# Two chained transformer blocks on one core: the fourth PSUM bank in the dense expert stage, the table store on GpSimd's queue, and the order of the first gates

## The chip, the cores and the metric

One core of one Trainium2 chip runs the whole program in a single launch. The metric is the device time of that launch in microseconds (us). All arithmetic is float32; products are made as three passes on values split into a high and a low part ("fp32r" in the rows).

## The reference, cut to what matters

Two blocks follow each other on 512 tokens of width 1024. The first has a gated linear attention branch, a sparse attention branch and a layer of 16384 experts (PEER); the second has a pooling mixer and a stick-breaking attention. The change lies in PEER:

```
s1, s2 = scores of q against 128 sub keys each
v1, i1 = top_k(s1, 16); v2, i2 = top_k(s2, 16)
best, ci = top_k(v1[..., :, None] + v2[..., None, :], 16)
expert_idx = ia * 128 + ib
gates = softmax(best)
u = expert_u[ix]; v = expert_v[ix]
a = gelu(einsum('td,thkd->thk', hx, u)) * gx
y = einsum('thk,thkd->td', a, v)
```

Each token thus uses 8 x 16 of the 16384 experts.

## The kernel before, in words

**Dense and sparse part.** For tokens 0 to 383 the expert layer is computed densely: all 16384 experts, as 128 chunks of 128 experts, with a table of gates that is zero where an expert wasn't chosen. For the last 128 tokens the chosen rows of `uv` are fetched by an indirect DMA and used on VectorE, one of 128 (head, rank) pairs at a time. The sparse part is called "rows" below.

**The gate table** (`peer_table`, lines 1414 to 1468). Four tokens at a time (a quad, 96 in all), VectorE and GpSimd make two one-hot matrices (L1422 to L1430), TensorE multiplies them (L1442), and ScalarE copies the 128 x 128 gates of each token into a stage of 64 tokens (L1445). A stage is 4 MB, 16 quads fill one, and there are six. Two buffers take turns, so a stage is written into the buffer of the one before the last. A full stage is stored to DRAM (`G`). The quads are made four items ahead of their product (`lag`). Between the quads stand hidden products whose results are stored for later ("spilled", `hidden` in the rows; L1485 copies one out of PSUM, ScalarE's queue stores it).

**The dense stage** (`peer`, lines 1634 to 1705). The chunks are worked in 32 groups of four. A chunk's gate step (`gate_chunk`, lines 1508 to 1524) applies Gelu to the hidden values in a PSUM bank (L1515 when they were spilled and are read from SBUF, L1518 when TensorE has just made them), multiplies by the gates (L1519), makes the high part (L1522), and later the low part (L1524, put off through `lowers`). Then eight output products (`peer_out`, lines 1530 to 1561), of twelve matmuls each, multiply the four chunks by `v`, and VectorE adds each to its sum (L1554 the first time, L1556 after). In most groups two of the four chunks are spilled and two are made on the spot, with 24 matmuls each; in groups 0, 6, 13, 19 and 26 all four are spilled. The outputs of a group are worked between the gate steps of the next one.

A row step (`step`, lines 1593 to 1609) goes with each chunk: L1600 adds a row's `v` part to a sum, `lowers` brings L1524, L1608 multiplies the next row's `u` part. Every third group has one step more. L1583 fetches the rows, two steps ahead, on GpSimd's queue.

**Banks.** Two PSUM tiles of two banks each hold the rows' operands in this stage. The others are 0, 1, 6 and 7. `self.ring(out=[...])` sets the list that `bank("out")` walks through in order, starting again at its first; a gate step and an output product each take the next. Before the change the list is 0, 1, 7 in the whole dense stage; bank 6 is used once, for chunk 6 (`early`).

**Order of the work.** Nothing is scheduled by the compiler: each engine runs its instructions in the order in which the items issue them, and waits where it needs data or a free buffer. `run` (lines 383 to 450) walks through the items. Ahead of each item it issues the casts of its weights and of `split_ahead` units behind them (L428 on ScalarE, the high part; L429, mostly on GpSimd, the low part), as far as there is room for three units, and right after each cast it issues the load of a following unit on SP's queue (two buffers). So a cast stands in ScalarE's order in front of the item that it was issued with, and a load stands in SP's order in front of the fetches that the item makes. `fetch_gates` (lines 1496 to 1506) loads a chunk's gates, and its spilled values, on SP's queue, four chunks ahead; it needs the whole table stored.

```
upto, n = last + 1, 0
while upto < len(units) and n < self.split_ahead:
    n += units[upto].split
    upto += 1
split(last + 1, upto)
...
it.fn(*[u.hl if u.split else u for u in it.units])
```

The transition goes like this: last quads and last table store, five more spilled products, `rows_banks` (row fetches 0 to 2) and `fetch_gates(4)` in front of them, then the product of chunk 6, the gates of chunks 0 to 3 and of chunk 6, then the first outputs.

Of the kernel before, what the change touches and what calls it, by code (L numbers as in the profile page):

```python
# [23 lines left out]
ND = NT - P  # L24
# [6 lines left out]
W = 64  # L31
# [258 lines left out]
def weave(main, fill):  # L290

    if not fill:
        return list(main)
    out = []
    tm = sum(i.cost for i in main) or 1.0
    tf = sum(i.cost for i in fill) or 1.0
    cm = cf = 0.0
    a, b = list(main), list(fill)
    while a or b:
        if a and (not b or cm / tm <= cf / tf):  # L300
            i = a.pop(0)
            cm += i.cost
        else:
            i = b.pop(0)
            cf += i.cost
        out.append(i)
    return out


class K:  # L310
# [1103 lines left out]
    def peer_table(self, first, fill):  # L1414

        nc, A = self.nc, self.A
        st = {}

        def quad(n):
            t0 = 4 * n  # L1420
            oa, ob = self.tmp(4 * P), self.tmp(4 * P)
            nc.vector.tensor_tensor(ob.v(4, P), self.iota[:, None, :].to_broadcast([P, 4, P]),  # L1422
                                    self.ibT.v(ND)[:, t0:t0 + 4, None].to_broadcast([P, 4, P]), op=OP.is_equal)
            if n % 2:
                nc.vector.tensor_tensor(oa.v(4, P), self.iota[:, None, :].to_broadcast([P, 4, P]),
                                        self.iaT.v(ND)[:, t0:t0 + 4, None].to_broadcast([P, 4, P]), op=OP.is_equal)
                nc.gpsimd.tensor_mul(oa.v(4, P), oa.v(4, P), self.gT.v(ND)[:, t0:t0 + 4, None].to_broadcast([P, 4, P]))
            for j in range(0 if n % 2 else 4):
                t = slice(t0 + j, t0 + j + 1)
                nc.vector.tensor_scalar(oa.v(4, P)[:, j], self.iota, self.iaT.v(ND)[:, t], self.gT.v(ND)[:, t],  # L1430
                                        op0=OP.is_equal, op1=OP.mult)
            st[n] = (oa, ob)

        def outer(n):
            oa, ob = st.pop(n)
            t0 = 4 * n
            if t0 == W:
                st["buf"] = A.wide.alloc(P * W, high=False, name="stage")
            stage = (st["buf"] if t0 // W % 2 else self.rows).v(P, W)
            ps = self.bank("out")  # L1440
            for j in range(4):
                nc.tensor.matmul(ps[:, j * P:j * P + P], lhsT=oa.v(4, P)[:, j], rhs=ob.v(4, P)[:, j], start=j == 0, stop=True,  # L1442
                                 skip_group_check=True)
            o = t0 % W
            nc.scalar.copy(stage[:, :, o:o + 4].rearrange("p b t -> p t b"), ps.rearrange("p (t b) -> p t b", b=P))  # L1445
            self.free(oa, ob)
            if o + 4 == W:
                self.load(self.G[:, t0 // W], stage, nc.scalar)
            if n == ND // 4 - 1:
                self.free(st["buf"])  # L1450
                self.free(self.gT, self.iaT, self.ibT)
                A.new_wide("split")

        items = []
        lag = 4
        for n in range(ND // 4 + lag):
            def fn(n=n):
                if n >= lag:
                    outer(n - lag)
                if n < ND // 4:  # L1460
                    quad(n)
            items.append(Item(fn, (), 0.9))
            if n == lag - 1:
                items += first
            if n >= lag and (n - lag) % 4 == 3 and n < ND // 4 and n - lag not in (27, 59):
                items += fill[:1]
                del fill[:1]
        return items + fill
# [165 lines left out]
    def peer(self, table, late):  # L1634
        nc, A = self.nc, self.A
        groups = P // 4
        ahead = []
        for gi in range(groups - 1):
            ahead += list(range(4 * gi, 4 * gi + (4 if gi in (0, 6, 13, 19, 26) else 2)))
        fresh = [c for c in range(P) if c not in ahead]  # L1640
        self.spilled = {c: i for i, c in enumerate(ahead)}
        self.order = []
        for gi in range(groups):
            self.order += [4 * gi + i for i in ((0, 2, 1, 3) if gi > 1 else (2, 0, 1, 3) if gi else range(4))]
        rows = self.dram.tile([P, P * ND + 1024], F32, name="gates")
        self.G = rows[:, :P * ND].rearrange("p (g b t) -> p g b t", b=P, t=W)
        self.H = self.dram.tile([len(ahead), P, ND], F32, name="hidden")
        self.g_bufs, self.act, self.g_next, self.lower = {}, {}, 0, []
        self.spare = []
        keys = self.peer_keys()  # L1650
        hid = self.peer_hidden(ahead, True)

        def begin():
            self.pacc = FRows(self, KB, name="pacc")

        def reload():
            self.x2 = FRows(self, KB, name="x2", slots=True)
            for i in range(KB):
                self.load(self.x2[:, i], self.X[i])
        n1 = len(ahead) - table  # L1660
        soft, turn = self.peer_gates()
        h = n1 - late
        items = weave(keys, hid[:h]) + hid[h:n1 - 4] + soft + hid[n1 - 4:n1 - 2]
        items.append(self.rings_at(hid=[6, 7], out=[0, 1, 2, 3, 4], att=[0, 1]))
        items += turn + self.peer_table(hid[n1 - 2:n1], hid[n1:])
        end = len(items) - 5
        items[end:end] = [self.rings_at(hid=[6, 7], out=[0, 1, 6, 7]), Item(self.rows_banks, (), 0.0),
                          Item(lambda: self.fetch_gates(4), (), 0.0)]
        items += [Item(begin, (), 0.0), Item(lambda: self.free(*self.spare), (), 0.0)]
        rest = dict(zip(fresh, self.peer_hidden(fresh, False)))  # L1670
        items += [self.rings_at(out=[6]), rest[6], self.rings_at(out=[0, 1, 7])]
        for c in range(4):
            items.append(Item(lambda c=c: (self.gate_chunk(c), self.lowers()), (), 0.0))
        items.append(Item(lambda: (self.gate_chunk(6, self.early), self.lowers()), (), 0.0))
        sparse = self.peer_rows()
        out = self.peer_out()
        pend = []
        for gi in range(groups):
            if gi == groups - 1:
                for a, b in sparse:  # L1680
                    items += [a, b]
                items.append(Item(reload, (), 0.0))
                sparse = []
            for i in range(4):
                c = self.order[4 * gi + i]
                n = 1 if gi else 0
                now, sparse = sparse[:n], sparse[n:]
                if c > 3 and c != 6:
                    items.append(rest[c] if c in rest else Item(lambda c=c: self.gate_chunk(c), (), 0.0))
                items += [a for a, _ in now] or [Item(self.lowers, (), 0.0)]  # L1690
                items += pend[2 * i:2 * i + 1]
                items += [b for _, b in now]
                items += pend[2 * i + 1:2 * i + 2]
                if i == 1 and gi and gi % 3 == 0:
                    items += sparse[0]
                    sparse = sparse[1:]
            if gi == groups - 1:
                items.append(Item(self.rows_end, (), 0.0))
            pend = out[gi]
        items += [self.split_by(nc.vector)] + pend  # L1700

        def end():
            self.free(self.pacc)
        items.append(Item(end, (), 0.0))
        return items
# [535 lines left out]
```

## Time and profile before

| | us |
|---|---|
| median of 3 runs | 2870.11 (2868.93 to 2875.13) |
| profiled execution, its own time | 2872.01 |
| its span, first to last instruction | 2870.3 |
| TensorE busy | 2706.1 (94%) |
| VectorE busy | 1746.1 (61%) |
| ScalarE busy | 1254.4 (44%) |
| GpSimd busy | 1609.4 (56%) |
| mean granted TensorE clock | 0.977 of full speed |

The span is cut into stages by what the engines do: up to 960 us the attention branches, the scores and the expert choice; 960 to 1130 the table; 1130 to 1185 the transition; 1185 to 2032 the dense stage; from then on the second block. PE is TensorE, DVE VectorE, ACT ScalarE, POOL GpSimd, SP SyncE; a q behind a name is that engine's instruction queue, where DMAs are issued. L1519 is line 1519 of the kernel; L380 is the helper that issues a DMA. An arrow reads "output tile<-input tiles"; in brackets stands the idle time of the engine before the instruction and what ended it.

### The profile page before, as it was taken

Reading aid. Unit: us, or ns where it says so; the run is one execution under the profiler, and the core shown is the slowest. Engines: PE = TensorE matmul, PEld = TensorE weight load, DVE = VectorE, ACT = ScalarE, POOL = GpSimd, SP = SyncE. Lnnn points to the kernel's source line nnn. Section 1 sums busy time; section 2 is a strip of 40 time slices with the busy share of each in tenths; the row PEclk is TensorE's granted clock in tenths of the full one; section 3 lists DMA queues with packets and bytes.
Section 4 is the critical chain, followed back from the end, with each engine's and each line's share of the span. In section 5 each row is a group of like instructions: output and inputs, shape, how many; then the busy total and the mean of one; then the engine's idle time right before and its main releaser. Section 6 shows DMA issues by size and latency. Waiting matters only on the chain.

```text
span 2870.3 us, 40036 instructions
## 1 busy us (share of the span) xinstructions
PE 2706.1 (94%) x14514; PEld 2443.0 (85%) x14514; DVE 1746.1 (61%) x3546; ACT 1254.4 (44%) x2507; POOL 1609.4 (56%) x1503
## 2 busy tenths in 40 slices
PE   6999999999999999798998989989999999999997
PEld 5897788888999999798998989889888887888896
DVE  6334576686888885466666676665584532444655
ACT  4344525534333575344443443434443234445543
POOL 3000334356777755476766667666655554766774
PEclk9999999999999999899999999999999999999998
DMA  6221221284344566789889898897323222221210
GB/s 245 89 74 59 88 78 41 81 324 146 134 148 141 193 242 241 255 315 332 315 312 336 299 326 327 302 342 253 118 87 118 88 103 74 74 74 59 74 59 30
DMA packets 187447, 502.19 MB, mean 175 GB/s; under 512 B 110192, under 2 KB 128752, under 8 KB 138864
## 3 DMA queue, kind: packets, MB, share of 16 engines
q1 hardware_dynamic: 151328, 305.04, 31.7%
q0 software_dynamic: 19072, 136.32, 11.7%
q10 hardware_dynamic: 16848, 58.27, 5.3%
q8 instruction: 114, 1.87, 0.3%
q14 instruction: 85, 0.70, 0.1%
HBM read 456.06 MB, written 43.52 MB: 174 GB/s over the span
## 4 chain that ended last, share of the span: by engine, by line
PE 38%; DMA 6%; DVE 5%; ACT 5%; POOL 3%; issue 2%; DVEq 0%; POOLq 0%; SPq 0%; ACTq 0%
PE bank L370 13%; PE bank L371 12%; PE bank L372 12%; DMA plain<-in_uv_dram,slot 5%; ACT split L428 2%; POOL split L429 2%; DVE bank L1600 1%; DVE bank L1519 1%; DVE plain L1608 1%; PE bank L2017 1%; PE bank L2016 1%; ACT bank L1518 0%; DVE slot L2001 0%; DVE slot L1556 0%; DVE wide L1524 0%
## 5 line engine op out<-in xcount | busy, mean ns | idle before, releaser
L429 POOL TENSOR_TENSOR split<-raw,split 128x512 fp32r<-128x512 f32 x856 | 1096.8, 1315 | 717.9 <-ACT split L428 637.5
L370 PE MATMUL bank<-slot,split 128*128 128x384 f32 (+2 forms) x1932 | 709.6, 367 | 38.8 <-DVE wide L1524 28.2
L371 PE MATMUL bank<-slot,split 128*128 128x384 f32 (+2 forms) x1932 | 703.1, 364 | 0.3 <-DVE slot L377 0.2
L372 PE MATMUL bank<-slot,split 128*128 128x384 f32 (+2 forms) x1932 | 702.8, 364 | 0.0
L370 PE MATMUL bank<-wide,split 128*128 128x384 f32 (+1 forms) x1688 | 620.7, 368 | 76.4 <-DVE slot L1556 27.6
L371 PE MATMUL bank<-wide,split 128*128 128x384 f32 (+1 forms) x1688 | 611.2, 362 | 2.2 <-POOL wide L629 2.2
L372 PE MATMUL bank<-wide,split 128*128 128x384 f32 (+1 forms) x1688 | 610.1, 361 | 0.0
L428 ACT CAST split<-raw 128x512 fp32r<-128x512 f32 x953 | 523.0, 619 | 138.2 <-PE bank L371 71.6
L370 PEld LDWEIGHTS bank<-slot,split 128*128 128x128 f32 (+1 forms) x1932 | 368.1, 191 | 82.1 <-DVE wide L1524 31.1
L370 PEld LDWEIGHTS bank<-wide,split 128*128 128x128 f32 x1688 | 323.7, 192 | 126.7 <-ACT slot L1605 23.3
L371 PEld LDWEIGHTS bank<-slot,split 128*128 128x128 f32 (+1 forms) x1932 | 368.2, 191 | 36.2 <-DVE slot L377 1.1
L372 PEld LDWEIGHTS bank<-slot,split 128*128 128x128 f32 (+1 forms) x1932 | 367.3, 190 | 36.1
L371 PEld LDWEIGHTS bank<-wide,split 128*128 128x128 f32 x1688 | 323.7, 192 | 30.6 <-POOL wide L629 3.4
L372 PEld LDWEIGHTS bank<-wide,split 128*128 128x128 f32 x1688 | 323.4, 192 | 26.9
L1519 DVE TENSOR_TENSOR bank<-bank,slot 128x384 f32<-128x384 f32 x128 | 72.0, 562 | 251.2 <-ACT bank L1518 197.5
L1608 DVE SCALAR_TENSOR_TENSOR plain<-plain,bank 128x1024 f32<-128x1024 f32 x128 | 155.3, 1213 | 80.4 <-DMA plain<-in_uv_dram,slot 80.3
L1583 POOL DMA_INDIRECT plain<-in_uv_dram,slot x128 | 121.3, 948 | 73.3 <-PE bank L371 30.1
L1600 DVE SCALAR_TENSOR_TENSOR bank<-plain,slot,bank 128x1024 f32<-128x1024 f32 x127 | 162.3, 1278 | 0.0
L1518 ACT ACTIVATE bank<-bank 128x384 f32<-128x384 f32 x56 | 26.6, 475 | 304.0 <-PE bank L372 304.0
L1522 ACT CAST wide<-bank 128x384 fp32r<-128x384 f32 x128 | 61.5, 480 | 172.9 <-DVE bank L1519 172.9
L1556 DVE TENSOR_TENSOR slot<-slot,bank 128x384 f32<-128x384 f32 x240 | 124.5, 548 | 15.9 <-PE bank L372 15.9
L429 DVE TENSOR_TENSOR split<-raw,split 128x512 fp32r<-128x512 f32 x97 | 66.2, 743 | 100.4 <-ACT split L428 100.4
(364 smaller groups left out, 3858.1 us busy)
## 6 DMA issues: line engine op xcount, KB each, us to landing
raw<-in_u_dram SPq DMA_DIRECT2D x64, 1024.0 KB, 5.1
raw<-in_v_dram SPq DMA_DIRECT2D x64, 1024.0 KB, 5.4
slot<-gates SPq DMA_DIRECT2D x128, 192.0 KB, 9.6
plain<-in_w_ada_dram ACTq DMA_DIRECT2D x32, 512.0 KB, 6.1
raw<-in_w_pool_dram SPq DMA_DIRECT2D x16, 1024.0 KB, 4.9
slot<-hidden SPq DMA_DIRECT2D x72, 192.0 KB, 10.4
gates<-plain ACTq DMA_DIRECT2D x3, 4096.0 KB, 13.4
gates<-wide ACTq DMA_DIRECT2D x3, 4096.0 KB, 13.0
```

The costliest lines, as they stand in the source:

```text
L370: mm(out, lhsT=w[0], rhs=x[0], start=start, stop=False, skip_group_check=True)
L371: mm(out, lhsT=w[0], rhs=x[1], start=False, stop=False, skip_group_check=True)
L372: mm(out, lhsT=w[1], rhs=x[0], start=False, stop=stop, skip_group_check=True)
L428: self.nc.scalar.copy(u.hl.hi[:, c], u.raw.v(u.n)[:, c])
L429: (u.lo or self.lo_engine).tensor_sub(u.hl.lo[:, c], u.raw.v(u.n)[:, c], u.hl.hi[:, c])
L1519: nc.vector.tensor_mul(ps, ps, b.v(ND))
L1522: nc.scalar.copy(a.hi, ps)
L1556: nc.vector.tensor_add(acc, acc, ps)
L1583: self.nc.gpsimd.indirect_dma_start(out=self.uvs[k % 4].rearrange("p a b -> p (a b)"), out_offset=None, in_=self.t["uv"], in_offset=bass.I ...
L1600: nc.vector.scalar_tensor_tensor(acc, v, a, acc, op0=OP.mult, op1=OP.add)
L1608: nc.vector.scalar_tensor_tensor(u, u, 1.0, self.hx, op0=OP.mult, op1=OP.mult, accum_out=self.dx.v(P)[:, k:k + 1])
L2016: mm(o, lhsT=w, rhs=s["L"][j].hi, start=False, stop=False, skip_group_check=True)
```

## The change

The store of a full stage moves from ScalarE's queue to GpSimd's and is issued three quads later (the last one at once). In the last six table items and up to the gates of chunk 6, weights are cast one unit ahead instead of two. The gates of chunks 0 to 3 are issued in front of the product of chunk 6. After the gates of chunk 6, bank 6 joins the list of the dense stage, which has four banks then.

```diff
             if o + 4 == W:
-                self.load(self.G[:, t0 // W], stage, nc.scalar)
+                st["full"] = (t0 // W, stage)
+            if o == 8 and t0 > W or n == ND // 4 - 1:
+                g, full = st["full"]
+                self.load(self.G[:, g], full, nc.gpsimd)
...
         rest = dict(zip(fresh, self.peer_hidden(fresh, False)))
-        items += [self.rings_at(out=[6]), rest[6], self.rings_at(out=[0, 1, 7])]
+
+        def ahead_by(n):
+            self.split_ahead = n
+        items.insert(end - 6, Item(lambda: ahead_by(1), (), 0.0))
+        items.append(self.rings_at(out=[0, 1, 7]))
         for c in range(4):
             items.append(Item(lambda c=c: (self.gate_chunk(c), self.lowers()), (), 0.0))
-        items.append(Item(lambda: (self.gate_chunk(6, self.early), self.lowers()), (), 0.0))
+        items += [self.rings_at(out=[6]), rest[6], Item(lambda: ahead_by(2), (), 0.0)]
+        items += [Item(lambda: (self.gate_chunk(6, self.early), self.lowers()), (), 0.0), self.rings_at(out=[0, 1, 6, 7])]
```

## Rows read from the trace of the kernel before

**Rows 1.** Windows by stage: length, busy us (instructions) of five engines, PEclk, DMA share, GB/s

```profile
960.00:1130.00 170.00, 169.76 (x1245) 169.57 (x1244) 139.43 (x315) 119.76 (x158) 106.66 (x95) 1.00 0.57 218
...
1130.00:1185.00 55.00, 37.37 (x186) 36.27 (x185) 9.97 (x19) 16.03 (x33) 17.02 (x15) 0.84 0.85 299
...
1185.00:2032.00 847.00, 774.71 (x4258) 754.30 (x4256) 543.17 (x878) 350.41 (x855) 563.59 (x478) 0.97 0.86 309
```

**Rows 2.** Timeline of TensorE in the transition: start us, us, instruction, [idle before <-releaser]

```profile
1155.52 0.69 PE L370 MATMUL bank<-slot,split 128*128 128x384 f32 x1 [4.58 <-ACT slot L1485]
...
1170.56 0.69 PE L370 MATMUL bank<-wide,split 128*128 128x384 f32 x1 [8.62 <-DVE wide L1524]
...
1180.85 0.69 PE L370 MATMUL bank<-wide,split 128*128 128x384 f32 x1 [4.43 <-DVE slot L1554]
```

**Rows 3.** Timeline of the other engines in the transition

```profile
1148.64 0.38 SPq L380 DMA_DIRECT2D slot<-gates  x1
...
1155.47 2.58 SPq L380 DMA_DIRECT2D raw<-in_v_dram  x2
...
1163.25 2.18 ACT L428 CAST split<-raw 128x512 fp32r<-128x512 f32 x4 [7.78 <-DMA raw<-in_v_dram]
...
1163.94 4.93 POOL L429 TENSOR_TENSOR split<-raw,split 128x512 fp32r<-128x512 f32 x4 [6.25 <-ACT split L428]
...
1168.90 0.33 SPq L380 DMA_DIRECT2D raw<-in_u_dram  x1
...
1177.52 0.57 DVE L1519 TENSOR_TENSOR bank<-bank,slot 128x384 f32<-128x384 f32 x1 [3.87 <-DMA slot<-gates]
```

**Rows 4.** The tile `gates` up to 1135 us: issue ns min/median/max, first and last start

```profile
L380 ACTq DMA_DIRECT2D gates<-plain x3: 326/326/327, 983.7 to 1099.1; - x3
L380 ACTq DMA_DIRECT2D gates<-wide x3: 326/326/327, 1010.4 to 1129.9; - x3
...
DMA to landing us min/median/max: 11.5/13.2/18.7
```

**Rows 5.** Waits of TensorE, 1185 to 2032 us: us in total, times, longest

```profile
PE bank L370 <- DVE wide L1524: 28.2, 9, 4.1
PE bank L370 <- DVE slot L1556: 27.6, 29, 5.1
PE bank L370 <- ACT bank L1515: 8.6, 25, 0.3
PE bank L370 <- ACT slot L1605: 6.8, 2, 5.4
```

**Rows 6.** Timeline of TensorE in ordinary groups of the dense stage

```profile
1203.64 0.33 PE L370 MATMUL bank<-slot,split 128*128 128x384 f32 x1
...
1207.80 0.33 PE L370 MATMUL bank<-wide,split 128*128 128x384 f32 x1
...
1281.76 0.41 PE L370 MATMUL bank<-wide,split 128*128 128x384 f32 x1 [0.34 <-ACT bank L1515]
...
1294.82 0.41 PE L370 MATMUL bank<-wide,split 128*128 128x384 f32 x1 [0.34 <-DVE slot L1556]
```

**Rows 7.** Timeline in a group with an extra row step, and in one without hidden products

```profile
1405.26 1.22 DVE L1608 SCALAR_TENSOR_TENSOR plain<-plain,bank 128x1024 f32<-128x1024 f32 x1 [2.59 <-DMA plain<-in_uv_dram,slot]
...
1408.67 0.45 PE L370 MATMUL bank<-slot,split 128*128 128x384 f32 x1 [3.11 <-DVE wide L1524]
...
1517.52 0.66 PE L370 MATMUL bank<-wide,split 128*128 128x384 f32 x1 [5.11 <-DVE slot L1556]
```

**Rows 8.** Windows right after two of the waits for L1524 (columns as in rows 1)

```profile
1408.60:1412.40 3.80, 3.73 (x12) 3.73 (x13) 2.08 (x5) 0.00 (x0) 0.77 (x1) 0.55 1.01 409
...
1492.40:1499.20 6.80, 6.70 (x25) 6.70 (x26) 2.12 (x5) 0.00 (x0) 0.81 (x1) 0.61 1.04 389
```

**Rows 9.** Line L1583, the row fetches: issue ns, who waited (us, times), landing us

```profile
L1583 POOL DMA_INDIRECT plain<-in_uv_dram,slot x128: 936/951/1069, 1127.9 to 1976.8; - x128
...
  DVE plain L1608: 80.3, 39
...
DMA to landing us min/median/max: 7.5/8.6/22.6
```

## Prediction, made before the changed kernel was run

> **What bounds the kernel now.** I first read busy time by stage [rows 1]. While the table is built TensorE is busy 169.76 of 170 us: whatever the change does there can cost time but give none. From 1130 to 1185 us it is busy 37.37 of 55 us, at a granted clock of 0.84. In the dense stage, 1185 to 2032 us, it is busy 774.71 of 847 us. So the change has two places to act: the transition, and 72 us of idle time plus some low clock in the dense stage.
>
> In the transition TensorE stands still three times [rows 2]: 4.58, 8.62 and 4.43 us. The other engines say why [rows 3]. The last 4 MB table store is issued at 1129.9 [rows 4]. The first gate fetch on SP, which needs it landed, goes out at 1148.64. Eight fetches take SP until 1155.47, and only then are the next weights (`w_v`) asked for. ScalarE meanwhile sits in front of the cast of those weights for 7.78 us, and the first Gelu comes after that cast. Then SP holds the fetch of the fifth gates behind a weight load (1168.90), and VectorE waits 3.87 us for it.
>
> In the dense stage nearly all waits are on a PSUM bank [rows 5]: 71.2 us in 65 waits. By the single waits, nine are for L1524 (28.2 us), four are long (5.4, 5.1, 4.5, 4.5), six are of 0.7 to 1.6 us (7.9 us), and 46 are of 0.34 us (15.6 us). Where ScalarE is named, a VectorE eviction ended at the same moment; I read those as bank waits too. The ring has three banks and a group takes twelve, so a product waits for the evacuation three takes earlier. With four it waits for the one four takes earlier. VectorE evacuates in take order, so every such wait moves to an earlier VectorE instruction: **no bank wait can become later through the ring itself.**
>
> **Part 1, the fourth bank.** Pitch: 24 matmuls from 1203.64 to 1207.80 us [rows 6], 4.16 us, so 0.173 us each, and a product of twelve holds a bank for 2.08 us. This is the slack that a fourth bank adds.
>
> *Short waits.* Two of them stand 13.06 us apart [rows 6] with 72 matmuls between (one hidden product, four outputs): 72 x 0.173 = 12.48, so one costs 0.58 us, with its restart, and at least its 0.34 of idle. The eviction it waits for stands in VectorE's order behind L1608, the row product. The one needed with four banks is the L1524 in front of it, or one eviction earlier. All 46 go: 46 x 0.5 = 23 us (16 to 27).
>
> *Waits for L1524.* Every third group has an extra row step. VectorE waits in it for its row (2.59 us), so the gate's L1524 comes late, and the hidden product that wants the gate's bank waits 3.11 us [rows 7]. With four banks that product wants a bank evicted two products before, and the gate's bank goes to an output 4.16 us later. All nine waits are at most 4.1 us, so all fit. The next row then comes late instead: between 0 and 2.08 us each, and I take 0.7, nearer to the lower end because most rows of this stage are there when wanted (39 waits in 128, rows 9). So 28.2 - 6.3 = 22 us. After such a wait the clock falls to its lower level, 1.2 of 2.4 GHz: a granted 0.55 over 3.80 us, or 0.61 over 6.80 [rows 8], which loses 1.7 or 2.7 us. Four of the nine waits are followed by the shorter kind and two by the longer: 4 x 1.7 + 2 x 2.7 = 12 us come back.
>
> *Long and middle waits.* The four long ones are in groups without new hidden products, where VectorE waits for a row (one is 5.11 us, rows 7). A bank buys 2.08 us of each, 8 us; the six middle ones go, 8 us. Together 16 us; I leave their clock as it is.
>
> *Given back.* Rows come by latency: 8.6 us from issue to landing, issued between weight casts on GpSimd [rows 9]. If the stage loses 73 us (23 + 22 + 12 + 16) in 124 rows, each row is wanted 0.6 us sooner. The 39 steps that already wait would wait 23 us more, and others that are just in time begin to. VectorE has slack for part of it: 0 to 35 us, and I take 18. The DMA share of 0.86 [rows 1] would rise to some 0.93, so transfers hide this no worse than now.
>
> Dense stage: 23 + 22 + 12 + 16 - 18 = **55 us**.
>
> **Part 2, the store.** Taken off ScalarE: six issues of 0.33 us, off the path. Put on GpSimd: six issues, at about the 0.95 us of a row fetch, in a stage where TensorE is at 100%. Five of them wait for nothing, because their buffer was full three quads before; behind each on GpSimd stand gate multiplies and casts, which shift by that microsecond. A buffer is written again one stage after its store. Stores are (1129.9 - 983.7) / 5 = 29.2 us apart [rows 4], three quads are 5.5 us, a landing is 11.5 to 18.7: covered. The last store waits on GpSimd for the last copy. The three row fetches queue behind it instead of being issued beside it; their first user, a row product, stands in VectorE's order behind four gates that need the same store, so that is free. The longest landing, 18.7 us, is that of the last store, beside those fetches; without them I expect 13 to 19 us, so landed at 1143 to 1149. Spilled products on ScalarE's queue no longer stand behind 4 MB.
>
> The Trainium skill (DMA: Bandwidth & Descriptors, Rules for kernel authors) says that spreading transfers over SP, ScalarE and GpSimd brings no bandwidth, since all run on the same 16 engines. By that rule the store would land no sooner, and part 3 would give 5 us instead of 10; the spread of 11.5 to 18.7 us [rows 4] shows that company matters, but no row has this store on GpSimd.
>
> **Part 3, the order.** With one unit cast ahead, the first `w_v` unit is asked for after the eight fetches. From the store's landing on: 6.8 us of fetch issues, 7.7 us for that load (1155.47 to its cast at 1163.25, rows 3), 0.7 for one quarter of its cast and 1.2 for the low part of it (4.93 us for four), 16.4 in all. TensorE restarts at 1159 to 1165 instead of 1170.56, a gain of 5.5 to 11.5. The first four gates are done on ScalarE meanwhile. Their fetches pull the fifth gates' in front of the weight load that held it, so the 4.43 us go too. The first stall, 4.58, also goes (the chunk's bank is free once ScalarE is not held up), but only lengthens the wait behind it. Against this stand two weight units cast in a row by GpSimd, later than now. Between 5 and 16 us; I take **10**.
>
> **Sum.** 55 + 10 = 65 us. The profiled execution took 2872.0 us with a span of 2870.3. This gives 2807.0 on its own time; the median of the runs shown is 1.9 lower, so **2805 us**. What a measurement of this kernel can tell from no change is about 0.2%, 5.7 us.
>
> **Rivals.**
> *The rows bind, not the banks.* The L1524 waits return whole, one product later, with their clock: 23 + 16 - 18 + 10 = 31 us, so 2839. For it: VectorE idles 80.3 us for rows [rows 9]. Against it: in an ordinary group the waits are short and stand behind the L1524 that counts.
> *ScalarE is the releaser after all*, as 27 of the 65 waits say, and the L1524 waits are for data, not for the bank. Then the change does less than it says: the 21 short L1556 waits and the transition, 10 + 10 us, so 2850. Against it: the product behind a late L1524 is a hidden product, which doesn't read that gate.
> *Slower: the store is slow from GpSimd.* Row fetches of 1 MB took up to 22.6 us beside a store. At 12 us per MB, between that and the median of 8.6, a store takes 48 us. It may take 29.2 - 5.5 + 1.8 = 25.5 before the next use of its buffer. Four stages then wait 22.5 us each, and the last store is 29 us later than now: 119 us, less 65, so 2924. It decides from 37 us on. Against it: issuing a row fetch took 936 to 1069 ns in all 128 cases [rows 9], beside a VectorE that was 64% busy.
> The Trainium skill (SBUF — State Buffer, Summary: rules for kernel authors) states this trap: descriptors written by GpSimd starve while VectorE runs in its faster modes, so such a transfer belongs on ScalarE's or SP's queue. By that rule the change would go this way; those 128 issue times show nothing of it.
>
> **How the numbers follow.** Forecast 0.62, rows 0.22, ScalarE 0.08, slow store 0.04, something unseen that leaves the time as it is 0.04. Of the first three nearly all is faster by over 0.2%: 0.91, same 0.05, slower 0.04. The forecast's own terms reach from 2870 - 90 = 2780 (nothing given back, 16 in the transition) to 2833 (35 given back, short waits at 0.34, 5 in the transition). With the rows' case the range goes to 2842.
>
> **What the next profile would show.** TensorE's waits for L1556 and L1524 in the dense stage fall from 71 to some 20 us, without the 13 us beat, and what is left stands in the groups without hidden products; that stage ends near 1967 us. VectorE's wait at L1608 rises above 80 us. The store lands within 19 us of its issue on GpSimd, the first Gelu stands in front of the cast of `w_v`, and the idle time of the transition falls from 17.6 to about 10 us. I am wrong if the long waits return one product later, if ScalarE's copies wait for a store, or if the row waits more than double.

## The result and the profile after

The changed kernel takes 2801.74 us (median of 4 runs, 2796.05 to 2804.61) against 2872.62 for the kernel before beside it (2868.93 to 2877.51, 4 runs): a ratio of 0.975, with a 95% interval of 0.9727 to 0.9773. Forecast were 2805 us and a range of 2780 to 2842. Its profiled execution took 2800.59 us, with a span of 2798.9. Up to line 1447 the line numbers are those of before; then three is added (L1556 is L1559, L1524 is L1527, the row product L1608 is L1611), and eight after line 1671.

First the windows by stage of the changed kernel, columns as in [rows 1]:

```profile
960.00:1130.00 170.00, 170.00 (x1246) 170.00 (x1245) 141.10 (x318) 116.63 (x153) 104.20 (x95) 1.00 0.57 217
1130.00:1185.00 55.00, 45.27 (x227) 42.80 (x227) 13.55 (x24) 23.02 (x46) 29.25 (x25) 0.88 0.84 295
...
1185.00:1961.00 776.00, 750.29 (x4226) 739.03 (x4225) 537.54 (x873) 346.54 (x847) 559.23 (x475) 0.98 0.94 337
```

The dense stage ends at 1961 us (2032 before, 1967 forecast), and TensorE is busy 97% of it. The DMA share is 0.94, 0.93 forecast. Its waits in that stage, against 71.2 us in 65 waits before [rows 5]:

```profile
PE bank L370 <- DVE slot L1559: 16.2, 12, 3.3
PE bank L370 <- DVE wide L1527: 8.7, 11, 4.4
```

25 waits for ScalarE of 0.34 us are gone, and with them the 13 us beat [rows 6]. VectorE's waits in the dense stage say where the time of late rows went. The kernel before:

```profile
DVE bank L1519 <- ACT bank L1518: 197.5, 54, 5.7
DVE plain L1608 <- DMA plain<-in_uv_dram,slot: 80.3, 39, 5.4
```

The changed kernel:

```profile
DVE plain L1611 <- DMA plain<-in_uv_dram,slot: 117.9, 66, 5.5
DVE bank L1522 <- ACT bank L1521: 111.1, 41, 4.1
```

VectorE waits 37.6 us more for rows and 86.4 us less for the products that TensorE has just made (ScalarE's Gelu, L1521, is named because it stands between the two). By this balance late rows have mostly eaten time in which VectorE would have waited for TensorE.

In the transition TensorE still stands still three times, but differently from [rows 2]:

```profile
1157.78 0.69 PE L370 MATMUL bank<-slot,split 128*128 128x384 f32 x1 [5.21 <-ACT slot L1488]
1168.00 0.41 PE L370 MATMUL bank<-wide,split 128*128 128x384 f32 x1 [3.50 <-DVE wide L1527]
1169.19 0.45 PE L372 MATMUL bank<-wide,split 128*128 128x384 f32 x1 [0.60 <-POOL split L429]
```

The idle time fell from 17.6 to 9.3 us; the 8.62 became 3.50 and the 4.43 went, but the first stall stayed. The other engines of the changed kernel in the transition, against [rows 3]; first GpSimd, SP, then ScalarE:

```profile
1131.82 0.58 POOL L380 DMA_DIRECT2D gates<-wide  x1 [7.42 <-ACT wide L1445]
1132.84 1.04 POOL L1586 DMA_INDIRECT plain<-in_uv_dram,slot  x1 [0.44 <-issue]
...
1135.45 0.94 POOL L1586 DMA_INDIRECT plain<-in_uv_dram,slot  x1 [0.30 <-issue]
...
1144.71 0.38 SPq L380 DMA_DIRECT2D slot<-gates  x1
...
1146.67 5.14 SPq L380 DMA_DIRECT2D slot<-hidden  x1
...
1156.30 0.86 SPq L380 DMA_DIRECT2D raw<-in_v_dram  x2
...
1157.25 0.48 ACT L1488 COPY slot<-bank 128x384 f32<-128x384 f32 x1 [8.32 <-DMA slot<-hidden]
1159.27 0.33 ACTq L380 DMA_DIRECT2D hidden<-slot  x1
1159.64 1.28 ACT L1518 ACT_TABLE_LOAD   x1 [1.91 <-DMA slot<-gates]
1160.93 0.49 ACT L1518 ACTIVATE bank<-slot 128x384 f32<-128x384 f32 x1
...
1167.16 3.22 ACT L428 CAST split<-raw 128x512 fp32r<-128x512 f32 x6
```

The store has landed when SP's first fetch goes out, 12.9 us after its issue (1131.82 to 1144.71; 18.7 before). But SP then needs 11.6 us for the eight fetches (1144.71 to 1156.30, where `w_v` is asked for) and needed 6.8; one issue alone took 5.14 us. ScalarE waits 8.32 us in front of the copy that TensorE's first stall is for.

**A ruler for all runs.** The part behind the dense stage, which no edit is aimed at, differs between profiled runs by as much as 10 us, so I compare the parts of one run. The transition is counted from the start of the last table copy (L1445) to that of the first addition of group 1 (L1556 or its shifted line), the dense stage from there to the last of the 240 additions, the rest from there to the end. All in us, from the starts of these instructions:

| profiled run | last copy at | transition | dense | rest |
|---|---|---|---|---|
| before | 1128.8 | 74.1 | 829.0 | 838.4 |
| changed | 1130.5 | 67.0 | 763.5 | 837.9 |
| e1 bank only | 1129.2 | 70.5 | 761.5 | 847.1 |
| e2 no bank | 1122.9 | 66.8 | 830.7 | 838.5 |
| e4 no store | 1126.9 | 63.1 | 763.0 | 840.0 |
| e5 no order | 1128.4 | 71.2 | 763.8 | 845.3 |
| e6 changed, again | 1129.4 | 66.6 | 763.9 | 843.0 |
| e7 rows first | 1130.5 | 60.9 | 763.4 | 840.4 |
| e8 rows moved | 1122.8 | 65.4 | 761.9 | 846.4 |
| e9 rows moved more | 1130.0 | 65.1 | 753.5 | 838.0 |
| e10 extra place | 1130.3 | 60.4 | 803.7 | 838.0 |
| e11 all moved | 1131.1 | 60.2 | 836.9 | 844.9 |
| e12 rows ready, before | 1130.7 | 73.5 | 763.6 | 836.8 |
| e13 rows ready, changed | 1123.3 | 66.9 | 721.4 | 838.6 |

So the change's 71.4 us of span are 65.5 in the dense stage, 7.0 in the transition, 0.5 in the rest, less 1.6 that it came later to the end of the table. Transition and dense stage are steady where kernels are alike: the changed kernel and its repeat, e6, have 67.0 and 66.6 us in the one, 763.5 and 763.9 in the other. The table itself takes 174.5 to 175.0 us in all fourteen, from its first copy (L1445) to its last, so the place of the store costs it nothing.

### The profile page after: what moved, and what is told of

Read it like the earlier page. It is cut to its first block, busy times and chain, and to the rows that moved or that the text cites. A ratio compares the mean times of both kernels' runs of the same rounds, so it can differ in the third digit from the quotient of the medians.

```text
span 2798.9 us, 39956 instructions
## 1 busy us (share of the span) xinstructions
PE 2688.3 (96%) x14514; PEld 2431.7 (87%) x14514; DVE 1744.2 (62%) x3546; ACT 1253.5 (45%) x2507; POOL 1612.9 (58%) x1509
## 4 chain that ended last, share of the span: by engine, by line
PE 63%; DMA 6%; DVE 4%; ACT 3%; issue 2%; POOL 2%; SPq 0%; DVEq 0%; ACTq 0%; POOLq 0%
PE bank L370 20%; PE bank L371 19%; PE bank L372 19%; DMA plain<-in_uv_dram,slot 5%; PE bank L1442 3%; POOL split L429 1%; PE bank L2025 1%; PE bank L2024 1%; ACT split L428 1%; PE bank L1281 1%; DVE slot L2009 0%; DMA gates<-wide 0%; SPq L380 0%; ACT plain L1995 0%; ACT plain L1994 0%
## 5 line engine op out<-in xcount | busy, mean ns | idle before, releaser
L370 PE MATMUL bank<-wide,split 128*128 128x384 f32 (+1 forms) x1688 | 617.4, 366 | 43.1 <-DVE slot L1559 16.2
L370 PEld LDWEIGHTS bank<-wide,split 128*128 128x128 f32 x1688 | 322.4, 191 | 86.4 <-DVE slot L1559 21.2
L1611 DVE SCALAR_TENSOR_TENSOR plain<-plain,bank 128x1024 f32<-128x1024 f32 x128 | 155.7, 1216 | 119.3 <-DMA plain<-in_uv_dram,slot 117.9
L1559 DVE TENSOR_TENSOR slot<-slot,bank 128x384 f32<-128x384 f32 x240 | 122.0, 547 | 2.8 <-PE bank L372 2.8
L1521 ACT ACTIVATE bank<-bank 128x384 f32<-128x384 f32 x56 | 26.6, 475 | 206.5 <-PE bank L372 206.5
```

Of the source, the lines that this page charges most:

```text
L370: mm(out, lhsT=w[0], rhs=x[0], start=start, stop=False, skip_group_check=True)
L1559: nc.vector.tensor_add(acc, acc, ps)
L1611: nc.vector.scalar_tensor_tensor(u, u, 1.0, self.hx, op0=OP.mult, op1=OP.mult, accum_out=self.dx.v(P)[:, k:k + 1])
```

## Experiments

### The three parts, one at a time

**e1**, the kernel before with the bank alone:

```diff
-            items.append(Item(lambda: (self.gate_chunk(6, self.early), self.lowers()), (), 0.0))
+            items += [Item(lambda: (self.gate_chunk(6, self.early), self.lowers()), (), 0.0), self.rings_at(out=[0, 1, 6, 7])]
```

> The kernel before with the fourth bank alone. Main theory: nearly the whole gain is the bank's and needs neither the store nor the order; in the two profiles the dense stage lost 65 to 66 us, so 2806 to 2810 us against some 2872 before, with the three idle times of the transition (4.58, 8.62, 4.43) as before. Rival: part of the dense stage's gain comes from the new order in front of it (weights and gates in another phase), then it stays above 2820 us.

Measured: 2810.06 us (ratio 0.9773, 0.9751 to 0.9795). The dense stage is 67.5 us shorter, the transition 3.5. Of the three idle times, expected as before, two are there (4.89 and 10.82 us) and the 4.43 is gone: it was a wait for a bank, and a fourth bank ends it.

**e2**, the changed kernel with `rings_at(out=[0, 1, 7])` in that place:

> The changed kernel with three banks in the dense stage. Main theory: only the transition's gain is left, 5 to 8 us, so 2864 to 2868 us, with TensorE's waits for the evictions and the low parts at some 70 us again and the 13 us beat back. Rival: the order alone already takes dense waits away, then below 2855 us.

Measured: 2868.07 us (0.9983, 0.997 to 0.9995). Its waits of TensorE from 1185 us on are those of [rows 5] again, the 25 of ScalarE among them:

```profile
PE bank L370 <- DVE slot L1559: 32.1, 30, 5.1
PE bank L370 <- DVE wide L1527: 27.4, 9, 4.1
PE bank L370 <- ACT bank L1518: 8.6, 25, 0.3
```

The dense gain is the bank's alone, and it needs neither of the other parts. The 25 waits come and go with the bank (e1 has none), so they are waits for a bank, though the profile names ScalarE. The 4.43 us are gone in e2 as well, without the bank: the new order ends that wait too, and the transition (66.8) is as short as with the bank.

**e4**, the changed kernel with the store of before; **e5**, with the order of before:

```diff
 e4
-                st["full"] = (t0 // W, stage)
-            if o == 8 and t0 > W or n == ND // 4 - 1:
-                g, full = st["full"]
-                self.load(self.G[:, g], full, nc.gpsimd)
+                self.load(self.G[:, t0 // W], stage, nc.scalar)
 e5
-        items.insert(end - 6, Item(lambda: ahead_by(1), (), 0.0))
-        items.append(self.rings_at(out=[0, 1, 7]))
+        items += [self.rings_at(out=[6]), rest[6], self.rings_at(out=[0, 1, 7])]
...
-        items += [self.rings_at(out=[6]), rest[6], Item(lambda: ahead_by(2), (), 0.0)]
```

> The changed kernel with the table stored as before (ScalarE's queue, at once). Main theory: the order brings the transition's gain and the store's queue matters little, so 2801 to 2805 us, with the last store landing within 2 us of where it lands in the changed kernel (12.9 us after its issue). Rival: the store's place is what frees ScalarE and its queue, then the gain of the transition falls away and it takes 2807 us or more.

> The changed kernel with the order and the casts of before (bank and store are new). Main theory: the cast of w_v stands in front of the first Gelu again, TensorE restarts near 1170 us with an idle time of 7 to 9 us, and the time is 2806 to 2810 us. Rival: the store alone brings the transition's gain, then 2800 to 2804 us.

Measured: e4 2791.87 us (0.9714, 0.9693 to 0.9736), lower than either theory had it, with the store landing 3.5 us later than in the changed kernel and not within 2; e5 2812.23 (0.9781, 0.9762 to 0.9799), 2 us above the main theory's figure. The cast of `w_v` stands in front of the first Gelu again in e5, but TensorE's wait ahead of the first output was 17.74 us, up to 1173.27, not 7 to 9. By the ruler the order brings 7.4 us beside the bank (transition 70.5 in e1, 63.1 in e4), and the store on GpSimd takes 3.9 of them back (63.1 to 67.0). Of the 10 us between the medians of e4 and the changed kernel only these 3.9 are seen in the parts that the edit touches; what else there is of it is not explained. e4 on SP and TensorE (its line numbers here are those of before):

```profile
1144.46 0.38 SPq L380 DMA_DIRECT2D slot<-gates  x1
...
1149.60 0.45 PE L370 MATMUL bank<-slot,split 128*128 128x384 f32 x1 [0.57 <-ACT slot L1485]
...
1150.89 0.81 SPq L380 DMA_DIRECT2D raw<-in_v_dram  x2
...
1161.32 0.66 PE L370 MATMUL bank<-wide,split 128*128 128x384 f32 x1 [7.28 <-DVE wide L1524]
```

The eight fetches take 6.4 us here and the first stall is 0.57. In e4 the three row fetches went out at 1121.02 to 1123.66, ahead of the store (1128.02), which landed after 16.4 us; in the changed kernel they queue behind it. That made the next question.

### Is it GpSimd's queue, or the three row fetches behind the store?

**e6** is the changed kernel again, beside **e7**, which issues the three row fetches ahead of the last store:

```diff
-        for k in range(3):
-            self.fetch_rows(k)
+
+    def rows_first(self):
+        for k in range(3):
+            self.fetch_rows(k)
...
+        items.insert(end - 4, Item(self.rows_first, (), 0.0))
```

> The changed kernel once more, beside the next three on the same chip. If the store through GpSimd costs some 4 us, as the transitions of the two profiles say (group 1 starts 7.0 us earlier than in the kernel before, counted from the end of the table, against 10.95 without it), 2797 to 2803 us; if the difference of 10 us between the medians was chance, it may come out below 2795 us.

> The changed kernel with the first three row fetches issued on GpSimd ahead of the last store, not behind it. Main theory: in the changed kernel those 3 MB collide with SP's fetches of the first gates; ahead of the store they don't, so the eight fetches take 6 to 7 us of SP's time and not 11.5, TensorE's wait for L1488 falls from 5.21 us below 1, and the time is 3 to 6 us below the changed kernel's in this call. Rival: a store on GpSimd's queue is itself what slows the fetches behind it; then the eight fetches take 10 us or more again and the time does not change.

Measured: e6 2803.61 us (0.9756, 0.9734 to 0.9778), e7 2796.84 (0.9729, 0.9704 to 0.9755). The medians are 6.8 us apart, 3 to 6 were expected, and the intervals of the two overlap a little; the ruler shows 5.7 us (66.6 to 60.9) in the transition and none in the dense stage. e7 on GpSimd, SP and TensorE:

```profile
1131.85 0.60 POOL L380 DMA_DIRECT2D gates<-wide  x1 [3.70 <-PE bank L1578]
...
1147.98 0.38 SPq L380 DMA_DIRECT2D slot<-gates  x1
1148.42 0.54 SPq L380 DMA_DIRECT2D slot<-hidden  x1
...
1153.17 0.45 PE L370 MATMUL bank<-slot,split 128*128 128x384 f32 x1 [0.57 <-ACT slot L1488]
...
1153.30 1.29 SPq L380 DMA_DIRECT2D raw<-in_v_dram  x2
...
1162.37 0.41 PE L370 MATMUL bank<-wide,split 128*128 128x384 f32 x1 [4.76 <-DVE wide L1527]
```

The store lands later (16.1 us after its issue, 1147.98), the eight fetches take 5.3 us, the first stall is 0.57 us, and TensorE restarts 14.4 us after the landing instead of 23.3. By the landings in the two traces the three rows are there at 1137.38 in e7, and SP's first fetch lands 2.8 us after its issue; in the changed kernel the rows land at 1148.73 to 1154.78, and that fetch needs 10.6 us. So it is the company, not the queue: 3 MB of rows delay what is in flight with them, the store in e7 and SP's fetches in the changed kernel. The first stall has a second cause, which e7 removes along with this one; it stands with the transition below. With the rows ahead of it, the store took 16.1 us from GpSimd (e7) and 16.4 from ScalarE (e4).

### What the rest of the dense stage's waits are for

**e12** and **e13** keep VectorE's work but fetch only four rows:

```diff
-        if k < P:
+        if k < 4:
...
-                nc.vector.scalar_tensor_tensor(u, u, 1.0, self.hx, op0=OP.mult, op1=OP.mult,
+                nc.vector.scalar_tensor_tensor(u, u, 1.0, self.hx, op0=OP.mult, op1=OP.add,
```

> The kernel before with only its first four row fetches (later steps use the rows that lie there, and add where they multiplied, so that the values stay finite): the sparse part's result is left out, VectorE's work is the same, no row is ever late, and 124 MB less are moved. The prediction's reading: the 46 short waits of the 13 us beat come from VectorE's order alone and stay (16 to 27 us); the nine waits for L1524 and the long ones come from late rows and go; so 2872 less 22 + 12 + 16 = 2822 us, 2812 to 2832. Rival: the waits for L1524 are the banks' even with rows on time; then above 2845 us.

> The same edit in the changed kernel. If what is left of the dense stage's waits (25 us in 24 waits, and 10 us of low clock) is late rows, they fall to under 5 us and the time is 25 to 35 us below the changed kernel's 2802, so 2767 to 2777 us; if it is the banks' or VectorE's, the time stays above 2790 us. Between this and e12 the fourth bank should still be worth the short waits, 23 us, and the transition 7.

Measured: e12 2810.79 us (0.98, 0.9776 to 0.9824), e13 2757.55 (0.962, 0.9598 to 0.9642). e12 is 1 us and e13 9 us below what was expected with late rows as the cause. TensorE's waits from 1185 us on in e12, where rows are never late and the banks are three:

```profile
PE bank L370 <- DVE slot L1556: 11.9, 31, 2.0
PE bank L370 <- ACT bank L1515: 8.6, 25, 0.3
...
PE bank L370 <- DVE wide L1524: 3.8, 9, 0.4
```

and in e13, with four:

```profile
PE bank L370 <- DVE slot L1757: 5.0, 2, 3.8
PE bank L370 <- DVE wide L1527: 1.1, 1, 1.1
```

The nine waits for L1524 fell from 28.2 to 3.8 us, so they were late rows; the short waits stayed, now 0.34 us every 13 us with hardly a break, so they are VectorE's order. In e13 one wait of 1.07 us is left in the whole dense stage (the line of L1757 lies behind it). By the ruler, late rows cost 65.4 us with three banks (829.0 to 763.6) and 42.1 with four; the bank is worth 65.5 with late rows and 42.2 without. The expectation had 23 us there, for 46 short waits; with the rows in time there are some 65 waits in the dense stage, nearly all of the short kind, and e13 has none of them. These two kernels also move 124 MB less, which this comparison can't take apart from the lateness.

### Can the rows be made less late?

Of the changed kernel's 24.9 us of waits, 17 stand in five places (1308.44, 1316.19, 1490.27, 1641.53, 1817.06), in the groups without hidden products. **e8** and **e9** take row steps out of those groups, on e4:

```diff
 e8
-                n = 1 if gi else 0
+                n = 1 if gi and not (gi in (6, 13, 19, 26) and i in (3,)) else 0
...
-                if i == 1 and gi and gi % 3 == 0:
+                if i == 1 and gi in (1, 3, 5, 8, 10, 12, 15, 16, 18, 21, 23, 25, 28, 30):
 e9
+                n = 1 if gi and not (gi in (6, 13, 19, 26) and i in (1, 3)) else 0
...
+                if i == 1 and gi in (1, 3, 4, 7, 8, 9, 11, 12, 15, 16, 18, 20, 22, 23, 24, 27, 28, 30):
```

> The kernel with the table stored as before (e4), and four row steps less in the groups without hidden products (3 each, 14 extra steps spread over ordinary groups). Theory: what is left of the dense stage's waits, five of 2.7 to 3.9 us in e4, stands in those groups because rows are asked for faster there than they come; then these waits fall to under 1 us each and the time is 10 to 16 us below e4's 2792, so 2776 to 2782 us. Rival: rows come late by the stage's total traffic (DMA share 0.94); then the waits only move to the groups with an extra step, and it stays above 2788 us.

> As e8, with two row steps in each group without hidden products and 18 extra steps. Theory: 0 to 3 us below e8, since little is left; rival: the extra steps now are what comes late, then 3 us or more above e8.

Measured: e8 2798.23 us (0.9754, 0.9732 to 0.9776), the rival's time but not its mechanism: its dense stage is e4's within 1.1 us, four of the five long waits stayed where they were (3.1 to 3.8 us), and the waits for L1524 did not grow (6.3 us, 7.7 in e4). e8 in group 6, on GpSimd, VectorE and TensorE:

```profile
1289.48 0.95 POOL L1583 DMA_INDIRECT plain<-in_uv_dram,slot  x1
...
1298.21 1.22 DVE L1608 SCALAR_TENSOR_TENSOR plain<-plain,bank 128x1024 f32<-128x1024 f32 x1 [3.82 <-DMA plain<-in_uv_dram,slot]
...
1299.96 0.44 PE L370 MATMUL bank<-wide,split 128*128 128x384 f32 x1 [3.16 <-DVE slot L1556]
```

The row is fetched two steps ahead and comes after 8.7 us; without hidden products two steps are 2 x 4.16 us. One step less at the end of the group changes nothing for the third. e9, with every other step gone, has what e8 lacked: 2791.66 us (0.9722, 0.9704 to 0.974), 6.6 below e8 and so beyond both of its expectations, with a dense stage 9.5 us shorter than e4's, and waits of TensorE from 1185 to 1949 us of

```profile
PE bank L370 <- DVE wide L1524: 15.7, 18, 3.2
PE bank L370 <- DVE slot L1556: 4.3, 8, 0.9
```

The evictions' waits fell from e4's 17.0 us to 4.3, and 8 us came back in the waits for L1524 (7.7 to 15.7). The 9.5 us are seen in one profiled run of each; the medians of e9 and e4 are the same (2791.66 and 2791.87).

**e10** put the extra step behind the first chunk's outputs, on e7; **e11** did that and e9's moves together:

```diff
 e10
-                if i == 1 and gi and gi % 3 == 0:
+                if i == 0 and gi and gi % 3 == 0:
 e11
+                n = 1 if gi and not (gi in (6, 13, 19, 26) and i % 2) else 0
...
+                if i == 0 and gi in (2, 4, 5, 7, 9, 10, 12, 14, 15, 17, 18, 20, 22, 23, 25, 27, 28, 30):
```

> e7 (row fetches ahead of the last store), with the extra row step of every third group put behind the outputs of the group's first chunk and not of its second. Theory: a row comes by latency (8.7 us from issue to use in the changed kernel's trace), so what counts is the space between steps; behind the second chunk no product lies between the extra step and the next one, behind the first there are 4.16 us on both sides. Then TensorE's waits for the low part of the gates fall, and the time is 3 to 8 us below e7's 2797, so 2789 to 2794 us. Rival: the rate of the rows counts, not their spacing; then as e7, 2795 to 2799 us.

> e10 with, besides, the row steps of e9: two in each group without hidden products, 18 extra steps in ordinary groups (none in group 1). Theory: e9 brought some 8 us in the dense stage by its trace and e7 some 6 in the transition, both on ways that do not touch each other; 2780 to 2787 us. Rival: the extra steps are now so many that each is late; then no better than e10.

Measured: e10 2839.71 us (0.99, 0.9881 to 0.9918), e11 2868.36 (0.9989, 0.9974 to 1.0004). For e10 neither figure came; for e11 the rival's did, no better than e10. e10 in a group with an extra step, on GpSimd, VectorE and TensorE (L1588 fetches the rows here, L1613 is the row product):

```profile
1375.10 0.95 POOL L1588 DMA_INDIRECT plain<-in_uv_dram,slot  x1 [0.15 <-issue]
...
1383.29 1.22 DVE L1613 SCALAR_TENSOR_TENSOR plain<-plain,bank 128x1024 f32<-128x1024 f32 x1 [5.41 <-DMA plain<-in_uv_dram,slot]
...
1384.44 0.56 DVE L1522 TENSOR_TENSOR bank<-bank,slot 128x384 f32<-128x384 f32 x1
...
1386.70 0.44 PE L370 MATMUL bank<-wide,split 128*128 128x384 f32 x1 [2.39 <-DVE wide L1527]
...
1389.23 1.22 DVE L1613 SCALAR_TENSOR_TENSOR plain<-plain,bank 128x1024 f32<-128x1024 f32 x1 [2.58 <-DMA plain<-in_uv_dram,slot]
```

The row product of the same group in e7:

```profile
1384.16 1.22 DVE L1613 SCALAR_TENSOR_TENSOR plain<-plain,bank 128x1024 f32<-128x1024 f32 x1 [2.64 <-DMA plain<-in_uv_dram,slot]
```

In both a row is used 8.2 us after it was asked for, so the latency of the theory held. But rows are fetched two steps ahead, and in its new place the extra step has less time behind its fetch: VectorE stands ready for it 2.8 us after the issue at 1375.10, in e7 5.6 us after. It waits 5.41 us instead of 2.64, and the step behind it, which waited for nothing in e7, waits 2.58 as well. Over all ten extra steps and the steps behind them these waits are 76 us in e10 and 29 in e7, and the dense stage is 40.3 us longer. Behind the late step in VectorE's order now stands, besides, the gate step of a chunk whose product TensorE has just made, in a bank that TensorE wants back; in the old place a spilled chunk follows. TensorE's waits for L1527 are 31.1 us in e10 and 9.0 in e7. How much of this is the place and how much the greater lateness was not taken apart.

## Why the prediction was right, and where it was not

- **Fourth bank, 55 us forecast, 65.5 measured.** I split the measured gain by the steps between TensorE's matmul starts from 1185 us to the end of the stage, counting what each exceeds 0.173 us by. Steps over 0.36 us: 84.7 us in 72 before, 31.2 in 31 after. Steps of 0.28 to 0.36 us, most of them at the lower clock (granted in them on average: 0.52 before): 18.5 us before, 9.9 after. Shorter steps: 7.2 and 3.7.
  - *Short waits, 23 us:* right. In e12 each cost 0.54 us (36.0 us in 67 steps, nearly all of this kind).
  - *Waits for L1524, 22 us:* 28.2 fell to 8.7, so 19.5. Their cause is shown by e12.
  - *Clock, 12 us:* 8.6.
  - *Long and middle waits, 16 us:* what is not L1524 and not short fell from 27.4 to 16.2 us, so 11. Three of the four long ones fell by 1.3 to 1.8 us each and not by 2.08. In group 6 nothing was gained: the 5.38 became 2.97, but 7.75 us behind it, about where 1.61 us stood, a wait of 4.42 came. The profile names L1527 for it; counted with the long ones it leaves 24 us for the waits for L1524 and 7 for this term. "No bank wait can become later through the ring itself" is not refuted by it, for with rows in time it is gone (e13), but with late rows a long wait did come back later there.
  - *"VectorE has slack for part of it: 0 to 35 us, and I take 18" was mis-sized, and is the step that failed.* Row waits rose by 37.6 us, more than the 23 I counted, yet the stage gained 65.5 of the 73 us that I had before this step: 7.5 us given back. They do not stand by themselves in the trace; they are what the terms above fall short of 73 by (some 11 us), less the 3.5 us of the shorter steps, which I had not counted. By the balance of VectorE's waits the slack was its wait for fresh gates (197.5 us), which I had not looked at.
- **Transition, 10 us forecast, 7.0 and 7.5 measured (changed, e6),** and by other steps than mine.
  - The store's landing at 1143 to 1149 us was right (1144.7), as were the first Gelu in front of the cast of `w_v` and the end of the 4.43 us, though the bank alone ends that wait too (e1).
  - "Their first user, a row product, stands in VectorE's order behind four gates that need the same store, so that is free" failed. It was true of the user and not of the engines: SP's fetches took 5 us longer with the row fetches in flight, and e7 gets that back.
  - "The first stall, 4.58, also goes" failed: 5.21. The trace tells for each DMA by which semaphore (a counter) its landing is told; 16 of them serve all. In the kernel before all 719 DMAs for which it can be told went out only after the landing of the one before on the same semaphore. In the changed kernel ScalarE's store of the fourth spilled product has the semaphore of SP's gate fetch of 1146.19. In front of that store ScalarE's queue waits for this semaphore; the fetch landed at 1156.74, the store went out at 1156.82. The store of the fifth has that of the fetch of 1154.93, which landed at 1159.20; it went out at 1159.27. So ScalarE stood behind SP's late fetches with no data between them, and the first Gelu came at 1160.93, 5 us after its hidden values (1155.92). In e4, e5 and e7 the fourth store has a semaphore that is free, and the stall is 0.57, in e5 with fetches as slow as here. In e7 the faster fetches and the other semaphore came together, and no run takes them apart.
  - TensorE restarted at 1168.00, not at 1159 to 1165, bound by the gates and no longer by the weights.
- **The sum** came out within 4 us of the median, 6 on the profiled runs, because the bank brought 10 us more than forecast and the transition 3 less, with a table that ended 1.6 us later and the rest of the span unchanged. That errors of both signs met is luck; the mechanism of the larger term, the bank, is shown by e1 and e2. Both mis-sized terms were inside the bounds I had written.
- **The rivals.** *Rows bind* (2839): no; the waits for L1524 did not return whole. But rows are what is left (e13: 42 us). *ScalarE as releaser* (2850): e1 and e2 rule it out. *Slow store from GpSimd* (2924): the stores took 582 to 614 ns to issue, and the last one 12.9 us to land; in e2, e5 and e13, whose traces have all six landings, they took 12.5 to 16.5 us. By the rule of the Trainium skill (SBUF — State Buffer, Summary: rules for kernel authors) GpSimd's descriptors starve while VectorE runs in its faster modes. No store here shows it, with VectorE busy 141 of the table's 170 us; in which mode VectorE ran, no row tells.
- **The rule on queues.** The Trainium skill (DMA: Bandwidth & Descriptors, Rules for kernel authors) says that another queue brings no bandwidth. The trace agrees: 16.1 us from GpSimd and 16.4 from ScalarE with the same fetches ahead (e7, e4). The transition gained by the order; moving the store lost 3.9 us until the row fetches were put ahead of it.

**Versions with medians below both kernels:** e4 (2791.87), e9 (2791.66) and e7 (2796.84). e4 is the change without its store; e9 adds the moved row steps, which its median does not show. The intervals of e7 and of the changed kernel overlap, and e4's just touches it; the ruler has e4 3.9 us and e7 6.1 us below the changed kernel in the transition. e9's steps with e7's fetches, leaving the extra step in its old place, were not run.

## What to carry to other kernels

A buffer more in a ring is priced by what evacuates it: sort the waits by the instruction that frees the buffer, and take each to the one before it in that engine's order. When a cheaper wait exposes a latency, look first at what the waiting engine was idle for anyway; only what exceeds that comes back as time. A DMA that nobody needs soon still costs those beside it, so ask what lands together and not only who waits for it, and look whether DMAs of two queues share the semaphore that tells of their landing. Before a step is moved whose data is fetched a fixed number of steps ahead, count the time between fetch and use in the new place, for it and for the step behind it.

## What was not expected of the hardware

- Issuing the second fetch of spilled values (192 KB) on SP's queue took 0.49 us in e7 and 5.14 in the changed kernel, with 3 MB of row fetches issued 11 to 14 us earlier; 5.14 to 5.92 us in all five kernels in which they went out behind the store. Rows are not the only company that does it: the fifth such fetch took 3.54 us in e7 (1156.65), with two weight loads just issued and the rows long landed.
- The landing of the 4 MB store goes by its company: 12.9 us with the three row fetches behind it in its queue, 16.1 and 16.4 with them ahead of it, 18.7 with them issued around it on another queue [rows 4].
- Stretches that the edits hardly touch differ between profiled runs by 8 us (up to the last table copy, 1122.8 to 1131.1) and 10 us (behind the dense stage, 836.8 to 847.1), so a difference of a few us between medians of five runs is better read from the part of the trace in which it should lie.
